# A two-layer decoder on one core: the order of the MLPs' products, the fetching of the modulation columns, operand offsets and a slot for raw weights

## The chip, the cores and the metric

The kernel runs on one core of one Trainium2 chip. The metric is the device time of one launch in microseconds (us). The engines are TensorE (PE, with its weight loads shown apart as PEld), VectorE (DVE), ScalarE (ACT), GpSimd (POOL) and SyncE (SP). SP only issues transfers, in strict order; POOL issues the transfers that add to what lies in SBUF already.

## The reference

One sequence of 512 tokens, model width 1024, two layers, everything in f32. Each layer modulates with six vectors that come from the conditioning vector `c`; layer 0 mixes with pooling windows, layer 1 with a gated unit (SGU); both end with an MLP of width 4096.

```python
c_act = jax.nn.silu(c)
for i in range(DEPTH):
    mod = c_act @ ada_w[i] + ada_b[i]
    sh1, sc1, g1, sh2, sc2, g2 = jnp.split(mod, 6, axis=-1)
    h = modulate(rmsnorm(x, norm_mix_g[i]), sh1, sc1)
    y = pool_mixer(h, ...) if i == 0 else sgu_mixer(h, ...)
    x = x + g1[:, None, :] * y
    h = modulate(rmsnorm(x, norm_mlp_g[i]), sh2, sc2)
    x = x + g2[:, None, :] * (jnp.square(jax.nn.relu(h @ mlp_w1[i])) @ mlp_w2[i])
return rmsnorm(x, final_g)
```

## The kernel before

**Split products.** TensorE works on f32r operands. Each f32 operand is split in a high part (`wh`, an ACT copy, L181) and a low part (`wl`, the rest, a DVE subtraction, L182), and each product is three matmuls: low by high, high by low, high by high (`mm3`, L194). So every weight block of 128 x 1024 costs one ACT and one DVE operation before PE can use it. Activations are split in the same way (L633 and L634).

**Seven products instead of eight.** Both matrix products of an MLP, M1 (`h @ w1`) and M2 (`... @ w2`), are cut in 2 x 2 blocks and computed in a Strassen-like way, with seven products numbered 1 to 7 in place of eight. Sums and differences of blocks are the operands. For the weights they are made one from another: a block `ch` (M1) or `bt` (M2) is loaded, split, then another block is added to it, and it is split again. DVE makes some of these additions (L742), the others are transfers that POOL issues (L738, L833). Results of the seven products are accumulated in PSUM, in two banks: 1, 6, 7, 4 in the X bank, 5 and 3 in the Z bank, 2 in a bank of its own (in M2, one that takes the Z bank's place once 3 is done). Between products of one bank, the sum so far has to be read out (L770 to L778 in M1). So product 4 may not begin before DVE has read the X bank after product 7 (L776).

**M1** runs over four columns `c` and two halves `j`. A unit `("s", (c, j, m))` is product m of group (c, j), 24 matmuls of 256 columns. Group (c, j) needs the blocks (0,0) (`ch`, slots T0 and T1), and (0,1), (1,1), (1,0) (`raw`, from the pool w4 with three buffers, which the modulation columns use too). The products run in the order 1, 5, 6, 3, 7, 2, 4, group after group, with the first groups interleaved. In layer 0 the first seven blocks of 128 columns, and block 7, are computed without this scheme while the normalisation is still running (the sweep).

**M2** runs over four blocks `c` of the hidden width. A unit `("p", (c, m))` is product m of block c: 24 matmuls of 512 columns, weights (stationary) from `o`, the split activations, and moving operands `wh`, `wl`. Here product m runs for c = 0..3 before the next m. Blocks: (0,0) is `bt`, (1,1) is `b` (slots P2, P3 in layer 0), (1,0) is `raw`.

**Order of the work.** PE follows the list `us` exactly. The other engines' instructions are traced up to five units ahead of the product that needs them (a unit of M2 counts as two) and then put in order by a scheduler, which moves them by its own estimates. `blk` loads a raw block when its product is BLK = 3 units ahead.

**Modulation columns.** `mod` is computed by columns: a 128 x 1024 tile `ada` of the weights is fetched (L210) and DVE multiplies it with the broadcast `c` and sums along the row (L214, one `ada_tile`). The gate of the MLP (eight columns) is turned to a row and broadcast by a trip through DRAM into `gb`, 128 x 1024 (`spread_cols`). In layer 0, 8 + 6 columns run during M1 through the slots T20 and T21, one every 2.2 products from the eighth on; ten more come during M2 through w4. In layer 1 eight columns are listed for M1. Fetch and use of a column are traced at the same place, and the scheduler may move both.

**Offsets.** Weight parts `wh`, `wl` lie at an address that is 192 modulo 512 bytes, activations at 128 modulo 512: `shift(big, 16)` puts 16 words between them. So in every product the two operands are 64 bytes apart.

```python
def shift(pool, words):
    if words % LINE:
        pool.tile([P, words % LINE], F32, name="shift", tag=f"shift{len(shifts)}", bufs=1)
```

Of the kernel before, what the change touches and what calls it, by code (L numbers as in the profile page):

```python
# [14 lines left out]
P = 128  # L15
# [12 lines left out]
PAD = 112  # L28

BLK = 3  # L30

EX = 6

EXW, EXE = 8, 2.2
# [49 lines left out]
def decoder_kernel(ctx: ExitStack, tc: tile.TileContext, xtok, vecs, rows, fgrow, ada0, adag, ada1, pool_w, w1s, w1f, w1b, w2, w_v, w_u, w_o, wsT, lnp, bs, out):  # L84
# [59 lines left out]
    gb = big.tile([P, D], F32, name="gb", tag="gb")  # L144
    shift(big, 16)
# [24 lines left out]
    def wtile(tag, dt=F32R):  # L170
        return wts.tile([P, D], dt, name=tag, tag=tag)

    def wpair():
        return wtile("wh"), wtile("wl")

    def split(r, n=1):

        h, l = wpair()
        for q in range(n):
            c = slice(D // n * q, D // n * (q + 1))  # L180
            A.activation(h[:, c], r[:, c], AF.Copy)  # L181
            V.tensor_tensor(l[:, c], r[:, c], f32(h[:, c]), ALU.subtract)  # L182
        return h, l
# [23 lines left out]
    def ada_tile(i, t, src, get):  # L207

        r = get()
        nc.sync.dma_start(r, src)  # L210
        b, j = divmod(t, 2)
        if j == 0:
            pmv[i, b] = sm.tile([P, 2], F32, name="pmv", tag="pmv")
        V.scalar_tensor_tensor(r, r, 1.0, cb, ALU.mult, ALU.mult, accum_out=pmv[i, b][:, j : j + 1])  # L214
# [17 lines left out]
    def spread_cols(cols, name):  # L232
# [7 lines left out]
        G.dma_start(gb, line.rearrange("(o k) p -> o (k p)", o=1).to_broadcast([P, D]))  # L240
# [25 lines left out]
    with (  # L266
# [90 lines left out]
        def load(name):  # L357
            kind, d = name.rstrip("0123456789"), [int(c) for c in name if c.isdigit()]
            for j, (pool, tag) in enumerate(places(name)):
                r = pool.tile([P, D], F32, name="ada", tag=tag) if pool is w4 else wtile(tag, F32)  # L360
# [255 lines left out]
    shift(late[0], PAD)  # L616

    ORDER = (1, 5, 6, 3, 7, 2, 4)
# [47 lines left out]
    def mlp(i, extra, wait, every, units, final):  # L666
# [5 lines left out]
        TS = ["T0", "T2", "T1", "R2"]  # L672
# [50 lines left out]

        def blk(c, j, r, n):
            if (c, j, r, n) not in blks:
                blks[c, j, r, n] = raw4(w1b[i, 2 * c + j, r, n], f"raw{c}{j}{r}{n}q")
            return blks[c, j, r, n]

        more = {}

        def s_prep(u):
# [14 lines left out]
            w = split(wb)  # L746
            if m == 6:
                add(t, *CHAIN[4])
            for at in more.get(u, ()):
                blk(*at)  # L750
            return w
# [36 lines left out]
        def t_load(c):  # L788
            if c == 3:
# [15 lines left out]

        def p_prep(u):
# [14 lines left out]
            o = slot(f"R{c % 2}", [P, 2, 4, 2, P], "o", F32R)  # L821
# [16 lines left out]
        XB, ZB = {}, {}  # L838

        def p_run(u, ready):  # L840
            c, m = u
            o, w = ready
            banks = XB if m in IN_X else ZB
# [5 lines left out]
            for n in range(8):  # L849
                p, hf = (n % 4, n // 4) if end else (n // 2, n % 2)  # L850
                wv = cut(w[p // 2], ALL, slice(S * (p % 2), S * (p % 2) + S))
                if (end and i and hf):
                    continue
                mm3(banks[hf], cut(o, ALL, p, hf), wv, start and p == 0, stop and p == 3, skip_group_check=True)
                if end and p == 3 and hf == 0:
# [15 lines left out]
            for hf in range(2):  # L871
# [5 lines left out]
                elif m in (3, 7):  # L877
                    with tc.high_priority():
                        V.tensor_tensor(yt, yt, banks[hf], ALU.subtract if m == 7 else ALU.add)
                else:  # L880
                    final(t, dh, 0, S, banks[hf], yt)
# [9 lines left out]
        ss_ = [u for k, u in units if k == "s"]  # L891
        need = {}
        for n, (c, j, m) in enumerate(ss_):
            for at in {2: [(c, j, 1, 0)], 5: [(c, j, 0, 1)], 6: [(c, j, 1, 1)]}.get(m, []):
                need.setdefault(at, n)
        for at, n in need.items():
            if n >= BLK:
                more.setdefault(ss_[n - BLK], []).append(at)
        real = [n for n, (k, u) in enumerate(units) if k in prep]
        ready = {}  # L900
        extra, n_s, total = list(extra), 0, len(extra)
        for n, (kind, u) in enumerate(units):
# [8 lines left out]
            for m in real[x:]:  # L911
                s += items[units[m][0]]
                if s > 5 and m != n:
# [3 lines left out]
            if kind == "s":  # L917
                n_s += 1
                while extra and n_s >= wait + every * (total - len(extra)):
                    extra.pop(0)()  # L920
# [4 lines left out]
    def gated(t, c0, n, src, y=None):  # L925
        tmp = sm.tile([P, S], F32, name="tmp", tag="tmp")[:, 0:n]
# [3 lines left out]
        V.tensor_tensor(tmp, src if y is None else y, gb[:, c0 : c0 + n], ALU.mult)  # L930
# [15 lines left out]
    def normed(hf, i, n):  # L946
# [13 lines left out]
        for k in range(0, KD, 2):  # L960
# [4 lines left out]
            tt = h32[k // 4][:, k % 4 : k % 4 + 2, c] if i and n else sm.tile([P, 2, 256], F32, name="tt", tag="tmp")  # L965
            for q in range(2):
                a, b = scl[i][n][:, k + q : k + q + 1], mod(i, c_sh(n, k + q))
                if q:
                    A.activation(tt[:, q], px[:, 256:512], AF.Identity, bias=b, scale=a)
# [9 lines left out]
    def p_units():  # L979
# [4 lines left out]
        us += [("p", (0, 2)), ("xl", (0,)), ("xl", (1,)), ("p", (1, 2)), ("sum", (0, 1)), ("sum", (1, 1)), ("p", (2, 2)), ("p", (3, 2))]  # L984
        us += [("p", (0, 4)), ("sum", (2, 1)), ("sum", (3, 1)), ("p", (1, 4)), ("p", (2, 4)), ("p", (3, 4))]
        return us

    def spread(i, name):
        return lambda: spread_cols(mods[i][:, c_g(1, 0) : c_g(1, 0) + KD], name)
# [5 lines left out]
    def ada_slot(t):  # L995
        return lambda: slot(f"T2{t % 2}", [P, D], "ada")

    ex = [lambda q=q: ada_tile(0, 40 + q, ada1[q], ada_slot(q)) for q in range(8)]
    ex += [lambda q=q: ada_tile(1, q, ada1[8 + q], ada_slot(q)) for q in range(EX)]
# [3 lines left out]
    us += s_units(2, 0, ORDER[1:]) + s_units(2, 1) + s_units(3, 0) + s_units(3, 1)  # L1003
    after(us, ("s", (2, 1, 2)), ("x", spread(0, "gain0")))
    after(us, ("s", (3, 1, 3)), ("tl", (0,)))
    us += p_units()
    after(us, ("p", (1, 4)), ("x", lambda: normed(0, 1, 0)))
    at = us.index(("p", (1, 5)))
    for q in range(EX, 16):
        us.insert(at + 1, ("x", lambda q=q: ada_tile(1, q, ada1[8 + q], get4)))  # L1010
        at += 2
    mlp(0, ex, EXW, EXE, us, lambda t, dh, c0, n, src, y: gated(t, S * dh + c0, n, src, y))
# [235 lines left out]
```

## Time and profile before

| | us |
|---|---|
| median of 3 runs (range) | 894.78 (888.55 to 895.37) |
| profiled execution | 896.06 |
| its span | 894.4 |

| stage | from, to (us of the span) |
|---|---|
| modulation and pool mixer | 0 to 60 |
| sweep, block 7 | 60 to 106 |
| M1 of layer 0 | 106 to 235 |
| M2 of layer 0 | 235 to 410 |
| SGU mixer, output projection last | 410 to 558 |
| M1 of layer 1 | 558 to 726 |
| M2 of layer 1 | 726 to 885 |

The mean granted clock of TensorE is 0.982. 188.62 MB are moved, 211 GB/s in the mean. The profile's rows are read so: a group's row has the line, engine, operation, out<-in and count, then busy time and mean duration; a row of waits has who waited for whom with total, times and longest; a row of the timeline has start, length, engine, line and operation, and in brackets the idle time before it and what ended it; a row of stretches has the busy time of each engine, the granted clock, the DMA share and GB/s.

### The profile page before, as it was taken

The page shows a single profiled execution, that of the slowest core. Times are in us where ns is not written, and L with a number is a line of the kernel's source. Part 1 is how long each engine was busy: PE and PEld are TensorE (multiplying, and loading weights), DVE is VectorE, ACT ScalarE, POOL GpSimd, SP SyncE. Part 2 cuts the span into 40 slices and gives each one's busy share as a digit, 9 for nine tenths or more (in the row PEclk, how much of TensorE's full clock was granted, in tenths as well). Part 3 has the DMA queues.
Part 4 walks back from the last instruction along what each step waited for, and adds up shares of the span by engine and source line. Part 5 has one row for each costly group of instructions (what it writes and reads, how often), then busy time and mean ns, then how long its engine had stood idle before and what let it go on. Part 6 is the DMA issues. An engine that isn't in the chain of part 4 may idle for free.

```text
span 894.4 us, 12710 instructions
## 1 busy us (share of the span) xinstructions
PE 845.1 (94%) x4895; PEld 738.2 (83%) x4895; DVE 693.5 (78%) x886; ACT 512.2 (57%) x732; POOL 110.5 (12%) x137
## 2 busy tenths in 40 slices
PE   8999999899849999999999989898999999999995
PEld 6778899899738888878888868898999998888884
DVE  5889789866939867687798975894766678966885
ACT  4286876567525555566331424774766675555661
POOL 3010010010213310020020001110101022311000
PEclk9999999999969999999999999999999999999998
DMA  9989969876999988336658864557566799998411
GB/s 343 407 329 309 303 150 264 256 208 198 292 264 204 202 191 206 121 105 242 209 191 272 282 224 164 166 136 194 148 153 183 198 252 223 206 195 188 165 48 47
DMA packets 51650, 188.62 MB, mean 211 GB/s; under 512 B 5739, under 2 KB 5891, under 8 KB 50566
## 3 DMA queue, kind: packets, MB, share of 16 engines
q1 hardware_dynamic: 37090, 133.52, 41.9%
q0 software_dynamic: 14352, 54.02, 31.4%
q8 instruction: 38, 0.62, 0.3%
q10 hardware_dynamic: 148, 0.27, 0.1%
q14 instruction: 22, 0.18, 0.1%
HBM read 181.49 MB, written 6.30 MB: 210 GB/s over the span
## 4 chain that ended last, share of the span: by engine, by line
PE 51%; DVE 20%; DMA 17%; ACT 5%; issue 4%; POOL 1%; SPq 1%; POOLq 0%; DVEq 0%; ACTq 0%
PE pm L194 29%; DMA ada<-in_ada 7%; DVE wl L182 5%; DVE ada L214 3%; PE po L194 3%; PE b211q L194 2%; PE b301q L194 2%; DMA wh<-in_ada 2%; PE b311q L194 2%; DMA ch10q<-in_w1b 2%; PE b201q L194 2%; ACT wh L181 2%; DVE ada L393 1%; PE b101q L194 1%; PE b111q L194 1%
## 5 line engine op out<-in xcount | busy, mean ns | idle before, releaser
L194 PE MATMUL pm<-wh,o 128*128 128x512 f32 (+1 forms) x904 | 284.4, 396 | 13.5 <-DVE o L634 13.0
L194 PEld LDWEIGHTS pm<-wh,o 128*128 128x128 f32 x904 | 171.1, 190 | 53.1 <-DVE o L634 13.4
L194 PE MATMUL pm<-wl,o 128*128 128x512 f32 (+1 forms) x452 | 179.1, 396 | 1.1 <-DVE wl L182 1.1
L634 DVE TENSOR_TENSOR o<-g,o 128x1024 fp32r<-128x1024 f32 x56 | 68.5, 1224 | 44.8 <-ACT o L633 44.6
L194 PEld LDWEIGHTS pm<-wl,o 128*128 128x128 f32 x452 | 85.8, 190 | 21.2 <-ACT tmp L935 1.5
L633 ACT ACTIVATE o<-g 128x1024 fp32r<-128x1024 f32 x56 | 59.3, 1058 | 71.5 <-PE pm L194 69.7
L214 DVE SCALAR_TENSOR_TENSOR ada<-ada,cb 128x1024 f32<-128x1024 f32 x56 | 67.9, 1222 | 34.2 <-DMA ada<-in_ada 34.0
L181 ACT ACTIVATE wh<-bt 128x1024 fp32r<-128x1024 f32 x64 | 67.3, 1054 | 32.9 <-PE pm L194 32.3
L182 DVE TENSOR_TENSOR wl<-bt,wh 128x1024 fp32r<-128x1024 f32 x64 | 78.5, 1236 | 5.2 <-ACT wh L181 5.1
L194 PE MATMUL po<-hb,wh 128*128 128x512 f32 x224 | 70.4, 395 | 0.0
L833 POOL DMA_DIRECT2D bt<-in_w x48 | 40.9, 852 | 130.0 <-DVE wl L182 124.1
L194 PEld LDWEIGHTS po<-hb,wh 128*128 128x128 f32 x224 | 42.1, 188 | 9.9
L182 DVE TENSOR_TENSOR wl<-raw,wh 128x1024 fp32r<-128x1024 f32 x33 | 40.2, 1223 | 8.6 <-ACT wh L181 8.6
L181 ACT ACTIVATE wh<-raw 128x1024 fp32r<-128x1024 f32 x33 | 34.7, 1053 | 19.6 <-DMA raw<-in_w_o 7.7
L194 PE MATMUL po<-hb,wl 128*128 128x512 f32 x112 | 44.8, 400 | 1.0 <-ACT g L696 1.0
L182 DVE TENSOR_TENSOR wl<-b,wh 128x1024 fp32r<-128x1024 f32 x32 | 39.0, 1222 | 5.3 <-ACT wh L181 5.3
L194 PE MATMUL po<-wh,gt 128*128 128x512 f32 x128 | 41.8, 405 | 0.0
L688 ACT ACTIVATE g<-g 128x512 f32<-128x512 f32 (+1 forms) x72 | 40.6, 596 | 1.3
L181 ACT ACTIVATE wh<-b 128x1024 fp32r<-128x1024 f32 x32 | 33.8, 1055 | 11.6 <-PE pm L194 11.0
L194 PE MATMUL po<-wh,hb 128*128 128x512 f32 x128 | 40.1, 392 | 0.0
L935 ACT ACTIVATE tmp<-x 128x512 f32<-128x512 f32 (+1 forms) x25 | 15.2, 608 | 40.9 <-DVE x L931 40.8
L780 ACT ACTIVATE g<-g 128x512 f32<-128x512 f32 x42 | 26.1, 622 | 20.1 <-DVE g L774 12.9
(438 smaller groups left out, 1992.8 us busy)
## 6 DMA issues: line engine op xcount, KB each, us to landing
ada<-in_ada SPq DMA_DIRECT2D x72, 512.0 KB, 4.7
bt<-in_w POOLq DMA_DIRECT2D x48, 512.0 KB, 9.1
bt<-in_w SPq DMA_DIRECT2D x16, 512.0 KB, 4.7
b<-in_w SPq DMA_DIRECT2D x16, 512.0 KB, 5.6
raw<-in_w SPq DMA_DIRECT2D x16, 512.0 KB, 4.3
b<-in_w POOLq DMA_DIRECT2D x16, 512.0 KB, 6.6
wh<-in_ada SPq DMA_DIRECT2D x9, 512.0 KB, 9.7
wl<-in_ada SPq DMA_DIRECT2D x9, 512.0 KB, 9.7
```

The lines of the kernel that those rows point to most:

```text
L181: A.activation(h[:, c], r[:, c], AF.Copy)
L182: V.tensor_tensor(l[:, c], r[:, c], f32(h[:, c]), ALU.subtract)
L194: T.matmul(o[:, c], a, b[:, c], start=first and q == 0 and not c.start, stop=last and q == 2 and c.stop is None, **kw)
L214: V.scalar_tensor_tensor(r, r, 1.0, cb, ALU.mult, ALU.mult, accum_out=pmv[i, b][:, j : j + 1])
L393: V.scalar_tensor_tensor(r, r, 1.0, cb, ALU.mult, ALU.mult, accum_out=out)
L633: A.activation(o[0], a, AF.Copy)
L634: V.tensor_tensor(o[1], a, f32(o[0]), ALU.subtract)
L688: A.activation(t, t, AF.Square)
L780: A.activation(t, t, AF.Relu)
L833: G.dma_start(r, piece(c, *nxt, q), accum_op=ALU.add)
L935: A.activation(tmp, xt, AF.Square, scale=D**-0.5, accum_out=s[:, len(cs) : len(cs) + 1])
```

## The change

1. *M2's order.* Product 2 is no longer behind 7 but spread over the list, with a bank of its own for all of M2 (`WB`); `o` takes the slots R0 and R1 in turn of use; loads of `b` move behind product 6 of block 1; block 2 of `bt` takes R2 and block 3 takes T1. Within a product the terms run high by high, low by high, high by low over all of a block's four pairs, not three terms pair by pair. The residual sums move.
2. *M1's order.* 1, 5, 6, 3, 2, 7 and then product 1 of the next group ahead of 4. In layer 1 the two halves of columns 0 and 1 alternate.
3. *Columns.* Fetch and use are two steps at given units: in layer 0 from unit 3 on, one every 1.8 units, used three units after the fetch (20 columns in M1, the last four from unit 61 on through w4); in layer 1 one every two units from unit 20 on. Both steps keep their place in the program's order.
4. *Raws in the gate row's slot.* Block (1,0) of a group, and in layer 1 (1,1) of two groups, goes to `gb`'s slot in place of w4. `spread_cols` takes the slot back during M2. LEAD = 4 in place of BLK = 3.
5. *Offsets.* The shifts between the pools go. Buffers of `wh`, `wl` have 64 words more, so they start at 128 or 384 modulo 512 bytes, the activations at 128; for M1 alone (`UNDER`) the weights lie 16 words further. So M2, the sweep and the mixer have their operands 0 or 256 bytes apart (modulo 512), M1 64 or 320.
6. Smaller: `tmp` has two buffers instead of three, the layers' second normalisations run at high priority and on ACT alone.

```diff
-PAD = 112
-BLK = 3
-EX = 6
-EXW, EXE = 8, 2.2
+UNDER = 16
+LEAD = 4
+EX = 12
+EXW, EXE, EXP, LAG, AHEAD = 3, 1.8, 61, 3, 5
...
-    gb = big.tile([P, D], F32, name="gb", tag="gb")
-    shift(big, 16)
+    gbs = [big.tile([P, D], F32, name="gb", tag="gb")]
...
-        return wts.tile([P, D], dt, name=tag, tag=tag)
+        return wts.tile([P, D + 64], dt, name=tag, tag=tag)
+    def wpair(at=0):
+        return tuple(wtile(tag)[:, at : at + D] for tag in ("wh", "wl"))
...
-    ORDER = (1, 5, 6, 3, 7, 2, 4)
+    ORDER = (1, 5, 6, 3, 2, 7)
...
+        def in_gb(c, j, r, n):
+            return ((r, n) == (1, 0) and (i, c, j) != (1, 0, 0)) or (i, r, n, j) == (1, 1, 1, 1) and c < 2
...
-            w = split(wb)
+            w = split(wb, 1, UNDER)
...
-            if c == 3:
+            if c == 2:
                 t = slot("R2", [P, 2, D], "bt")
...
-            for n in range(8):
-                p, hf = (n % 4, n // 4) if end else (n // 2, n % 2)
+            if not end:
+                for q in range(2):
+                    for n, (a, b) in enumerate(((0, 0), (1, 0), (0, 1))):
+                        for p in range(2):
+                            for hf in range(2):
+                                T.matmul(banks[hf], o[a][:, 2 * q + p, hf], w[q][b][:, S * p : S * p + S], start=start and q + n + p == 0, stop=stop and q + n + p == 4, skip_group_check=True)
...
-        us += [("p", u) for u in ((0, 3), (1, 3), (0, 7), (1, 7), (2, 3), (3, 3), (2, 7), (3, 7))]
-        after(us, ("p", (1, 5)), ("bl", (0,)), ("bl", (1,)))
+        us += [("p", u) for u in ((0, 3), (1, 3), (1, 2), (0, 7), (1, 7), (2, 3), (3, 3), (2, 2), (2, 7), (3, 7), (3, 2))]
+        us.insert(4, ("p", (0, 2)))
+        after(us, ("p", (1, 6)), ("bl", (0,)), ("bl", (1,)))
...
+            def fetch(src=src, tag=tag, r=r):
+                r.append(slot(tag, [P, D], "ada") if tag else get4())
+                tc.keep_in_program_order(nc.sync.dma_start(r[0], src))
+            def column(i=i, t=t, r=r):
+                ada_column(i, t, r[0], tc.keep_in_program_order)
+            extra.setdefault(int(when(n)), []).append(fetch)
+            extra.setdefault(int(when(n)) + (LAG if tag else 2), []).insert(0, column)
```

What it makes of the engines' orders is shown at three places. The first is DVE at the seam from M1 to M2 of layer 0, where the first `o` (low part of the first M2 operand) stands. Before:

```order
L214 SCALAR_TENSOR_TENSOR ada_2654,pmv_2656<-ada_2654,cb_104 128x1024
L182 TENSOR_TENSOR wl_2223<-raw3110q_2128,wh_2222 128x1024
L214 SCALAR_TENSOR_TENSOR ada_2661,pmv_2656<-ada_2661,cb_104 128x1024
L182 TENSOR_TENSOR wl_2258<-ch31q_1503,wh_2257 128x1024
L199 TENSOR_TENSOR mods1_90<-pmv_2656,vec_78 128x2
L214 SCALAR_TENSOR_TENSOR ada_2669,pmv_2671<-ada_2669,cb_104 128x1024
L203 SCALAR_TENSOR_TENSOR scl10_93<-mods1_90,vec_78 128x1
L634 TENSOR_TENSOR o_2317<-g_898,o_2317 128x1024
L182 TENSOR_TENSOR wl_2321<-bt_2313,wh_2320 128x1024
```

And now:

```order
L181 TENSOR_TENSOR wl_2270<-ch31q_1516,wh_2269 128x1024
L217 SCALAR_TENSOR_TENSOR ada_2176,pmv_2273<-ada_2176,cb_104 128x1024
L181 TENSOR_TENSOR wl_2335<-bt_2327,wh_2334 128x1024
L638 TENSOR_TENSOR o_2402<-g_896,o_2402 128x1024
L791 TENSOR_TENSOR g_1719<-b315q_2243,g_1719 128x512
L638 TENSOR_TENSOR o_2331<-g_896,o_2331 128x1024
L181 TENSOR_TENSOR wl_2340<-bt_2328,wh_2339 128x1024
L793 TENSOR_TENSOR g_1791<-g_1791,b311q_2178 128x512
L217 SCALAR_TENSOR_TENSOR ada_2241,pmv_2273<-ada_2241,cb_104 128x1024
```

Three columns stood in a row of seven operations ahead of the first `o`; now one stands ahead and one behind it.

The second is SP's queue at the same seam (`b` is the block of products 3 and 7, `bt` of the others, `raw` of product 2). Before:

```order
L795 DMA bt_2498<-in_w2 128x1024 x2
L795 DMA bt_2458<-in_w2 128x1024
L210 DMA ada_2711<-in_ada1 128x1024
L210 DMA ada_2757<-in_ada1 128x1024
L210 DMA ada_2799<-in_ada1 128x1024
L210 DMA ada_2842<-in_ada1 128x1024
L804 DMA b_2658<-in_w2 128x1024 x2
L804 DMA b_2666<-in_w2 128x1024 x2
L210 DMA ada_2884<-in_ada1 128x1024
L210 DMA ada_2929<-in_ada1 128x1024
L210 DMA ada_2971<-in_ada1 128x1024
```

And now:

```order
L166 DMA raw_3000<-in_w2 128x1024
L1037 DMA ada_2241<-in_ada1 128x1024
L812 DMA bt_2474<-in_w2 128x1024 x2
L812 DMA bt_2405<-in_w2 128x1024
L812 DMA bt_2515<-in_w2 128x1024
L812 DMA bt_2406<-in_w2 128x1024
L821 DMA b_2875<-in_w2 128x1024 x2
L821 DMA b_2878<-in_w2 128x1024 x2
L166 DMA raw_3006<-in_w2 128x1024
L821 DMA b_3048<-in_w2 128x1024 x2
L821 DMA b_3087<-in_w2 128x1024 x2
L1037 DMA ada_3166<-in_ada1 128x1024
```

Seven column fetches stood among these blocks; now one stands ahead of them and the next behind all four loads of `b`.

The third is DVE at the output projection of the SGU mixer (`po` is its PSUM bank, `wl` the split of its weights; ada_5605 and up are the eight columns of layer 1's MLP gate, ada_4495 and ada_4494 the last one of the mixer's own). Before:

```order
L182 TENSOR_TENSOR wl_4574<-raw_4571,wh_4573 128x1024
L1091 TENSOR_TENSOR gt_4410<-u_3991,gt_4410 128x512
L214 SCALAR_TENSOR_TENSOR ada_5670,pmv_5607<-ada_5670,cb_104 128x1024
L214 SCALAR_TENSOR_TENSOR ada_5740,pmv_5742<-ada_5740,cb_104 128x1024
L199 TENSOR_TENSOR mods1_90<-pmv_5607,vec_78 128x2
L214 SCALAR_TENSOR_TENSOR ada_5811,pmv_5742<-ada_5811,cb_104 128x1024
L930 TENSOR_TENSOR tmp_4490<-po_4446,gb_105 128x512
```

And now:

```order
L181 TENSOR_TENSOR wl_4573<-raw_4570,wh_4572 128x1024
L1132 TENSOR_TENSOR u_3989<-po_4402,u_3989 128x512
L1131 TENSOR_TENSOR po_4412<-po_4412,wsbs_3629 128x512
L1137 TENSOR_TENSOR gt_4409<-u_3989,gt_4409 128x512
L1132 TENSOR_TENSOR u_3989<-po_4412,u_3989 128x512
L1137 TENSOR_TENSOR gt_4409<-u_3989,gt_4409 128x512
L951 TENSOR_TENSOR tmp_4489<-po_4445,gb_4132 128x512
```

The gate's columns are gone from this place; they stand in layer 1's M1 now.

More of the change, by code (lines that the diff above doesn't have):

```diff
@@ L895, in mlp @@
                 need.setdefault(at, n)
+        spare[:] = [at for at in need if in_gb(*at)]
         for at, n in need.items():
-            if n >= BLK:
-                more.setdefault(ss_[n - BLK], []).append(at)
+            if not in_gb(*at):
+                more.setdefault(ss_[max(n - LEAD, 0)], []).append(at)
         real = [n for n, (k, u) in enumerate(units) if k in prep]
         ready = {}
-        extra, n_s, total = list(extra), 0, len(extra)
         for n, (kind, u) in enumerate(units):
@@ L916, in mlp @@
                     ready[m] = prep[units[m][0]](units[m][1])
[L917 to L920, printed above, removed]
+            for f in extra.get(x, ()):
+                f()
             run_[kind](u, ready[n])
@@ L1147, in last1 @@
             nc.sync.dma_start(out[t, :, 0], xt[:, 0:S])
-    ex = [lambda q=q: ada_tile(1, 40 + q, ada1[48 + q], ada_slot(q)) for q in range(8)]
+    ex = columns([(1, 40 + q, ada1[48 + q], f"T2{q % 2}") for q in range(8)], lambda n: 20 + 2 * n)
     def h_late():
```

133 lines of the change are left out of this document (78 added, 55 removed).

## The prediction

> **What bounds the kernel now.** I read the page first, for the engine that is busiest, then the table of stretches, to see in which stages that engine is not busy.
>
> ```profile
> PE 845.1 (94%) x4895; PEld 738.2 (83%) x4895; DVE 693.5 (78%) x886; ACT 512.2 (57%) x732; POOL 110.5 (12%) x137
> ```
>
> ```profile
> 106.00:235.00 129.00, 121.54 (x1012) 120.22 (x1011) 106.62 (x133) 86.73 (x125) 13.01 (x16) 0.97 0.79 229
> 235.00:268.00 33.00, 20.04 (x83) 16.09 (x83) 17.34 (x24) 11.30 (x13) 5.70 (x7) 0.80 0.97 267
> 268.00:395.00 127.00, 127.00 (x545) 102.89 (x544) 101.80 (x103) 73.57 (x81) 23.54 (x25) 1.00 0.76 173
> 560.00:726.00 166.00, 158.62 (x1343) 157.57 (x1343) 120.80 (x120) 115.36 (x161) 19.50 (x23) 0.99 0.66 174
> 726.00:872.00 146.00, 146.00 (x630) 118.32 (x628) 114.87 (x111) 86.58 (x96) 26.27 (x31) 1.00 0.77 178
> ```
>
> The columns are the stretch, its length, then busy time and count of PE, PEld, DVE, ACT and POOL, the granted PE clock, the DMA share and GB/s. TensorE is the bound. In M2 (268 to 395 and 726 to 872) it never stops. It stops in M1 of both layers (106 to 235, 560 to 726) and hardest at the seam between M1 and M2 of layer 0 (235 to 268), where the clock falls too. So I look next at what PE waits for, and what DVE waits for.
>
> ```profile
> PE pm L194 <- DVE o L634: 13.0, 1, 13.0
> PE b201q L194 <- DVE g L776: 3.1, 1, 3.1
> ...
> PE b011q L194 <- ACT g L770: 2.7, 1, 2.7
> PE b311q L194 <- DVE g L776: 2.6, 1, 2.6
> PE b101q L194 <- ACT g L770: 2.6, 2, 2.3
> PE po L194 <- DVE wl L182: 2.5, 1, 2.5
> PE px L964 <- ACT xs L952: 2.1, 2, 1.7
> PE b012q L194 <- ACT h L969: 2.0, 1, 2.0
> ```
>
> ```profile
> DVE ada L214 <- DMA ada<-in_ada: 34.0, 14, 14.3
> ...
> DVE ch10q L742 <- DMA raw1011q<-in_w1b: 4.9, 1, 4.9
> DVE ch11q L742 <- DMA raw1111q<-in_w1b: 4.5, 1, 4.5
> ```
>
> Each row is who waited for whom: total us, times, longest. PE's longest waits are for DVE or ACT; DVE's own longest waits are for transfers, and an engine that waits holds everything behind it. A wait also costs after it has ended, since the clock is low for a while:
>
> ```profile
> 169.00:173.00 4.00, 3.96 (x20) 3.96 (x21) 4.00 (x7) 3.95 (x6) 0.00 (x0) 0.57 0.79 224
> 231.00:235.00 4.00, 4.00 (x22) 4.00 (x23) 4.00 (x7) 3.30 (x5) 0.85 (x1) 0.60 1.08 223
> 264.50:268.50 4.00, 3.62 (x9) 2.90 (x10) 4.00 (x8) 0.00 (x0) 1.71 (x2) 0.52 0.58 164
> 534.00:538.00 4.00, 3.75 (x9) 2.83 (x10) 4.00 (x6) 0.64 (x1) 0.00 (x0) 0.57 0.71 250
> 571.00:575.50 4.50, 4.50 (x26) 4.50 (x27) 3.61 (x6) 3.44 (x7) 0.20 (x1) 0.63 0.82 154
> ```
>
> At the usual 0.113 us (M1) or 0.233 us (M2 and the mixer) a matmul, these 20, 22, 9, 9 and 26 matmuls would take 2.3, 2.5, 2.1, 2.1 and 2.9 us. The low clock therefore costs about 1.7, 1.5, 1.5 (after 0.4 us of the wait that still lies inside), 1.7 and 1.5 us.
>
> The Trainium skill, page "TensorE: Matmul & The Clock Gate", section "HAM oscillation — how this bites in real kernels", says that the clock is throttled by idle gaps longer than about 3.4 us. By that rule only the 13.0 us wait would cost clock, the other four drops would stay, and the sum below would end about 4 us higher, near 866. The rows speak against it: the clock is at 0.57 to 0.63 after waits of 3.1, 2.6, 2.5 and 2.0 us.
>
> **The change part by part.** The sum is made against the profiled execution's 896.1 us (its span of 894.4 and 1.7 around it). That is 1.3 us above the median, and I leave this difference out.
>
> *The seam of layer 0 (columns fetched early and pinned).* The timeline of DVE there:
>
> ```profile
> 243.56 2.47 DVE L182 TENSOR_TENSOR wl<-bt,wh 128x1024 fp32r<-128x1024 f32 x2
> 245.95 0.15 DVE L203 SCALAR_TENSOR_TENSOR scl<-mods,vec 128x1 f32<-128x1 f32 x1
> 260.38 1.23 DVE L214 SCALAR_TENSOR_TENSOR ada<-ada,cb 128x1024 f32<-128x1024 f32 x1 [14.28 <-DMA ada<-in_ada]
> ...
> 263.60 1.22 DVE L634 TENSOR_TENSOR o<-g,o 128x1024 fp32r<-128x1024 f32 x1
> ```
>
> ```profile
> 237.14 5.72 SPq L210 DMA_DIRECT2D ada<-in_ada  x3
> ```
>
> SyncE issues the last three ada transfers only from 237.1, behind four w2 blocks for product 3, and DVE sits on one of them for 14.28 us; the low part `o`, for which PE waits 13.0, is two ada columns behind it. In the new order two columns stand at this seam, fetched before those blocks, and the last four come eighteen products later. The wait has nothing left to wait for: 13.0 plus 1.5 of clock. What is late next is the first low part itself. M2's new term order needs it only after the four matmuls of the high parts, so I keep 0.5 us and take **-14**. If the cover fails (a column that is late again), up to the whole 14 comes back.
>
> *M1 of layer 0.* Here the waits are not for transfers but for DVE's turn:
>
> ```profile
> 165.43 0.68 DVE L774 TENSOR_TENSOR g<-b205q,g 128x512 f32<-128x512 f32 x1
> 166.03 1.22 DVE L214 SCALAR_TENSOR_TENSOR ada<-ada,cb 128x1024 f32<-128x1024 f32 x1
> ...
> 167.17 1.22 DVE L182 TENSOR_TENSOR wl<-ch21q,wh 128x1024 fp32r<-128x1024 f32 x1
> 168.30 0.68 DVE L776 TENSOR_TENSOR g<-g,b201q 128x512 f32<-128x512 f32 x1
> ```
>
> PE may start product 4 only when L776 has read product 7 from the same bank, and two long operations are ahead of it. The change spaces the columns evenly, fetches each three products before its use, and puts two products instead of one between 6 and 7 (between 7 and 4 it stays one). That removes at most 3.1 + 2.6 and 0.3 (b101q's shorter wait) plus 1.7 + 1.5 of clock, 9.2. But the load stays: 106.62 us of DVE in a stretch that would shrink from 129 to about 120, or 89%. At such a load some evictions are late still; I take two thirds, **-6**. The other side: at 1.22 us a column, two more than now in this stretch, uncovered, are +2.5.
>
> *The gate row's slot for M1's raws, and the new product order in M1 of layer 1.*
>
> ```profile
> ACT wh L181 <- DMA ch10q<-in_w1b: 7.7, 2, 4.9
> ...
> ACT wh L181 <- DMA ch01q<-in_w1b: 4.7, 1, 4.7
> ```
>
> ACT waits 4.7 and 4.9 us at a split for a block to which GpSimd's transfer is still adding, DVE at the same time 4.9 and 4.5 us for a raw, and the copies that free PE's bank stand behind these splits: PE waits 2.7 and 2.3. A fourth buffer for raws (the gate row's) and a lead of four products instead of three bring the raws earlier. Interleaved pairs of groups put six or seven products instead of three between product 6, which starts the addition, and product 4, which needs it. I take 4.5 of these 5.0. The start of this stage (b012q 2.0, 1.5 of clock) gets the normalisation at high priority, but both halves of it on ACT: half, 1.7. Together **-6.2**. In exchange eight columns of 1.22 us come into this stage; DVE has 120.80 of 166, so 45 us of room hide them. Without that cover they would cost 10.
>
> *The mixer's output projection.* The first of the same eight columns now stand in front of it, hoisted there:
>
> ```profile
> 523.52 1.23 DVE L214 SCALAR_TENSOR_TENSOR ada<-ada,cb 128x1024 f32<-128x1024 f32 x1 [4.35 <-DMA ada<-in_ada]
> ```
>
> They delay the split that `po` waits for (2.5, then 1.7 of clock). With them gone from there I take **-4**.
>
> *M2's product order.* Both M2 stretches show PE busy throughout, so the order of products and of the terms within one can gain nothing inside them: **0**. The cover is DVE's slack, 25 of 127 us in the one and 31 of 146 in the other; w2 blocks for product 2 are loaded earlier, but each still has several products of 5.6 us. At the end of layer 0's M2 the normalisation now stands ahead of two residual sums; the px row's 1.7 us is there, and I take **-1.2**.
>
> *The address offset.* Profile rows cannot show a pair of operands at the same offset: in the kernel before, every product has 64 bytes between them. They do show that the pace isn't one number:
>
> ```profile
> 236.00:251.00 15.00, 15.00 (x67) 12.33 (x66) 0.00 (x0) 0.00 (x0) 1.00 1.05 274
> 270.00:394.00 124.00, 124.00 (x533) 100.42 (x532) 3.83 (x6) 3.60 (x6) 1.00 0.75 172
> ...
> 107.00:126.00 19.00, 19.00 (x164) 1.00 0.68 190
> 175.00:227.00 52.00, 52.00 (x460) 1.00 0.74 209
> 628.00:683.00 55.00, 55.00 (x469) 1.00 0.63 166
> ```
>
> ```profile
> 35.65 3.62 PE L470 MATMUL po<-pw,pd 128*128 128x256 f32 x16
> ```
>
> The first two rows are M2's own matmuls (512 columns): about 0.229 us each ahead of the long wait (one or two of the 67 straddle the edges) and 0.233 behind it. The next three, 256 columns in M1, give 0.116, 0.113 and 0.117: about 4% between two paces at the same offsets, and the pace changes only where PE has stood. The last row, of two-pass f32, has 15 steps in 3.62 less 0.38 for the last one's tail, 0.216 a step. The offset changes for some 1,344 matmuls of M2 (56 products of 24) and 768 in the sweep and the mixer. Bounds: all at 0.216 would give 2,112 x 0.017 = -36 us; a loss twice as large as the one that 0.233 has against 0.216 would give +36. I stay near M2's own rows and count only that fewer long waits leave more of it at the faster pace: **-2**.
>
> The Trainium skill, page "SBUF — State Buffer", section "Who interferes with whom", gives the streamed operand and the weight load two independent read ports. By that the offset cannot matter, this term is 0, and the sum is 864; no run here shows it yet.
>
> Sum: 14 + 6 + 6.2 + 4 + 1.2 + 2 = 33.4; 896.1 - 33.4 = 862.7, so **862**.
>
> **The rivals.** *Only the seam and the projection are won.* For it speaks DVE's 89%: M1's evictions may wait as before, and pinned columns can no longer slide behind them. Against it, the stretch of 175 to 227 ran without a wait. It gives 896 - 14 - 4 = 878, up to 888 if two added columns and a slow pace (+4% of 100 us) come on top.
>
> *The common offset is the faster one.* At 0.226 a step (twice M1's fast 0.113) 2,112 matmuls save 15 instead of 2: 849; at 0.216 it is 828. For it: a slow pace exists and nothing else in the rows explains it. Against: M1 keeps its 64 bytes and has both paces.
>
> *The common offset collides (the slower side).* If a weight load and a stream that start in step disturb each other, each of the 2,112 steps pays. The price decides from 33.4 / 2,112 = 0.016 us, 7% of a step. At +0.017 the time is 900, and with M1 not improved, 914. Against it: the two paces differ by half of that.
>
> *The change doesn't do what it says:* the columns' transfers could still wait in SyncE's queue behind blocks whose slots DVE must free. Then the seam stays and the time is near 885.
>
> **How the numbers follow.** Forecast (850 to 876) 0.60; seam and projection only 0.14; fast offset 0.11; collision 0.12; queue as before 0.03. The range takes in the fast offset's nearer half and the partial win: 842 to 888; outside remain the far half of the one and most of the collision. About 1% (9 us) is what a measurement of this kernel can tell from no change. Faster by more: forecast, fast offset, nearly all of the partial win, 0.82. Within 1%: a mild collision and the rest, 0.07. Slower: 0.11.
>
> **What would show it.** Right: no DVE wait for ada above 2 us between 100 and 250; PE's wait for the first `o` under 1 us and no low clock there; no wait of `po` for `wl` in the projection; raw waits in layer 1 gone; M2 still without a gap. Wrong: M2's 533 or so matmuls in 124 us become fewer than 510 or more than 560 (the offset), or L776's successor ends waits of 2 to 3 us in M1 again (DVE's load).

## The result, and the profile after

The changed kernel takes **860.65 us** in the median (857.71 to 864.85, four runs), the kernel before 893.88 in the runs beside it: a ratio of 0.9642, 95% interval 0.9581 to 0.9703. The forecast was 862. The profiled execution took 864.85 (span 863.1) and is the slowest of the four; the one of before, 896.06, lay 2.2 above its median. Their difference is 31.2, against a sum of 33.4.

The first line of the page after, and the stretches that answer to those shown of before (columns as there: PE, PEld, DVE, ACT, POOL, clock, DMA share, GB/s):

```profile
PE 836.9 (97%) x4895; PEld 737.4 (85%) x4895; DVE 690.0 (80%) x878; ACT 514.9 (60%) x740; POOL 117.9 (14%) x137
```

```profile
106.00:226.50 120.50, 118.59 (x1009) 117.99 (x1008) 108.11 (x137) 85.07 (x124) 11.20 (x13) 1.00 0.85 252
226.50:250.00 23.50, 21.65 (x95) 17.29 (x94) 15.03 (x13) 13.33 (x15) 5.26 (x7) 1.00 1.04 262
250.00:372.00 122.00, 120.39 (x529) 98.56 (x529) 100.36 (x103) 72.57 (x81) 23.41 (x26) 1.00 0.81 194
372.00:392.00 20.00, 17.08 (x71) 14.04 (x70) 15.02 (x20) 12.77 (x19) 8.33 (x3) 0.83 0.66 226
...
534.00:575.00 41.00, 36.48 (x303) 35.50 (x302) 34.35 (x38) 34.54 (x53) 4.68 (x5) 1.00 0.45 118
575.00:700.00 125.00, 125.00 (x1064) 125.00 (x1063) 96.26 (x103) 86.86 (x118) 12.98 (x15) 1.00 0.84 230
700.00:842.00 142.00, 142.00 (x628) 117.47 (x628) 114.17 (x109) 85.20 (x95) 27.74 (x33) 1.00 0.78 183
```

The seam (235 to 268 before, now 226.5 to 250) has lost its hole: PE stands 1.85 us in it where it stood 13. Up to 842 the clock is 1.00 but for one stretch, 372 to 392. M1 of layer 1 stands only in its first 41 us. New is that M2 of layer 0 has gaps (120.39 of 122, then 17.08 of 20). By stages, with the boundaries of the table ahead and those of the new trace (106, 226.5, 391.7, 534.4, 699.9, 853.9):

| stage | before | after | change | forecast (offset shared out by steps) |
|---|---|---|---|---|
| M1 of layer 0 | 129 | 120.5 | -8.5 | -6 |
| M2 of layer 0 | 175 | 165.2 | -9.8 | -15.8 |
| SGU mixer | 148 | 142.7 | -5.3 | -4.5 |
| M1 of layer 1 | 168 | 165.5 | -2.5 | -6.2 |
| M2 of layer 1 | 159 | 154.0 | -5.0 | -0.6 |

The waits of PE, and then those of DVE and ACT for transfers:

```profile
PE pm L874 <- DVE o L638: 3.1, 3, 1.4
PE px L985 <- ACT xs L973: 2.9, 2, 2.4
PE b001q L193 <- DVE wl L181: 1.6, 1, 1.6
PE b002q L193 <- DVE sums L960: 1.6, 1, 1.6
...
PE b101q L193 <- DVE g L793: 1.2, 1, 1.2
```

```profile
DVE ada L217 <- DMA ada<-in_ada: 3.1, 4, 1.1
...
DVE ch11q L757 <- DMA raw1111q<-in_w1b: 2.6, 1, 2.6
DVE ch10q L757 <- DMA raw1001q<-in_w1b: 2.4, 1, 2.4
...
ACT wh L180 <- DMA raw<-in_w: 0.7, 1, 0.7
```

DVE's waits for columns fell from 34.0 (longest 14.3) to 3.1 (1.1). No wait of `po` for `wl` is left. The raws' waits are halved, not gone. The normalisation's wait (`px`) at the end of layer 0's M2 grew from 1.7 to 2.9 (2.4, then 0.6), and it is what costs clock:

```profile
375.60:382.40 6.80, 6.23 (x23) 0.51 0.59 207
537.00:541.00 4.00, 2.40 (x21) 1.00 0.87 328
```

After the 2.4 us wait the clock is at half for 6.8 us, which costs about 3 (eight matmuls of M2 take 3.27 us there and 1.98 at full clock); after the wait of 1.6 us at 537 it stays at 1.00. But the length of a wait doesn't decide it. Four of the kernels below have the same pair of waits at this place (2.3 to 2.4 us, then 0.6 or 0.7): behind it the clock was at half for 6.8 us (M1 at 128 bytes), for 3.4 (the offset undone; M1's old order in layer 1) or not at all. This is the stretch of the last one, M1 at 0 or 256 bytes; its 15 transposes `px` took 1.86 us there, 3.46 in the changed kernel:

```profile
376.00:383.00 7.00, 6.22 (x35) 1.00 0.72 237
```

In the kernel before, too, waits of 2.7 and 2.3 us in M1 of layer 1 left the clock at 1.00. The rule of the Trainium skill that the prediction weighed ("TensorE: Matmul & The Clock Gate", section "HAM oscillation — how this bites in real kernels": idle gaps over about 3.4 us) would have no loss in this kernel; the row of 375.60 above is against it.

### The profile page after: what moved, and what is told of

Its sections match the earlier page's. It is cut to its first block, busy times and chain, and to the rows that moved or that the text cites. A ratio compares the mean times of both kernels' runs of the same rounds, so it can differ in the third digit from the quotient of the medians.

```text
span 863.1 us, 12746 instructions
## 1 busy us (share of the span) xinstructions
PE 836.9 (97%) x4895; PEld 737.4 (85%) x4895; DVE 690.0 (80%) x878; ACT 514.9 (60%) x740; POOL 117.9 (14%) x137
## 4 chain that ended last, share of the span: by engine, by line
PE 58%; DVE 19%; DMA 12%; issue 5%; ACT 4%; POOL 1%; SPq 0%; POOLq 0%; DVEq 0%; ACTq 0%
PE pm L874 28%; PE po L193 6%; DVE wl L181 4%; DVE ada L217 3%; PE b211q L193 3%; PE b301q L193 3%; DMA wh<-in_ada 2%; PE b201q L193 2%; PE b311q L193 2%; DMA ada<-in_ada 2%; DVE ada L397 2%; ACT wh L180 1%; PE b111q L193 1%; PE b205q L193 1%; PE b305q L193 1%
## 5 line engine op out<-in xcount | busy, mean ns | idle before, releaser
L874 PE MATMUL pm<-wh,o 128*128 128x512 f32 x864 | 216.1, 392 | 3.8 <-DVE o L638 3.1
L874 PEld LDWEIGHTS pm<-wh,o 128*128 128x128 f32 x864 | 162.4, 189 | 39.6 <-DVE o L638 4.3
L874 PE MATMUL pm<-wl,o 128*128 128x512 f32 x432 | 115.7, 389 | 0.1
L874 PEld LDWEIGHTS pm<-wl,o 128*128 128x128 f32 x432 | 81.0, 188 | 17.4 <-DVE wl L181 0.5
L181 DVE TENSOR_TENSOR wl<-raw,wh 128x1024 fp32r<-128x1024 f32 x33 | 40.2, 1221 | 14.3 <-ACT wh L180 14.2
```

Source lines behind the costliest of these rows:

```text
L874: T.matmul(banks[hf], o[a][:, 2 * q + p, hf], w[q][b][:, S * p : S * p + S], start=start and q + n + p == 0, stop=stop and q + n + p == 4, ...
```

## The experiments

Theory to begin with: the sum of the prediction, except that its offset term is too small, since M2's steps now have one steady pace (745 to 820, PE busy throughout: before 323 matmuls, after 332).

**The offset undone, and the offset alone.**

```diff
-    def wpair(at=0):
+    def wpair(at=16):
...
-    def split(r, n=1, at=0):
+    def split(r, n=1, at=16):
```

> The changed kernel with one thing undone: all weight parts lie 16 words further again, so that M2, the sweep and the mixer have 64 or 320 bytes between their operands (modulo 512), as M1 has. Theory (the common offset gives M2 its steady 0.2267 us a step): M2 and the mixer go back to 0.229 to 0.233 a step, and 2,100 steps at 0.0025 to 0.0065 more give 866 to 874 us instead of 861. Rival (the pace comes from the new term order, or from PE no longer standing before M2): still 0.2267 a step, 861 us.

> The kernel before with part 5 of the change alone (and two buffers of tmp instead of three, to make room): operands of M2, the sweep and the mixer 0 or 256 bytes apart, M1 at 64 or 320. Theory: 0.2267 a step in M2 and the mixer instead of 0.233, 10 us less, 884 us, with PE's waits for the first o (13.0) and for wl (2.5) still there. Rival (the pace comes from the new term order or the missing long wait): 0.233 behind the 13 us wait as before, 893 us.

```diff
-    shift(big, 16)
...
-        return wts.tile([P, D], dt, name=tag, tag=tag)
...
+        return wts.tile([P, D + 64], dt, name=tag, tag=tag)
...
-    shift(late[0], PAD)
...
-            w = split(wb)
+            w = split(wb, 1, 16)
```

Measured: undone, 861.31 us (858.58 to 866.25; 0.9665 of before, 0.9600 to 0.9731); alone, 890.15 (0.9972, 0.9942 to 1.0002). The theory fell in its time: no difference in the first, and at most 5 us in the second, perhaps nothing. The paces it speaks of are there, though. The same stretches of before and of the offset alone (M2 alone), of the offset undone, and after:

```profile
745.00:820.00 75.00, 75.00 (x323) 1.00 0.99 199
```

```profile
745.00:820.00 75.00, 75.00 (x332) 1.00 0.99 205
```

```profile
165.00:220.00 55.00, 55.00 (x487) 1.00 0.87 284
585.00:680.00 95.00, 95.00 (x841) 1.00 0.85 242
...
745.00:820.00 75.00, 75.00 (x329) 1.00 0.76 182
```

```profile
165.00:220.00 55.00, 55.00 (x469) 1.00 0.89 274
585.00:680.00 95.00, 95.00 (x809) 1.00 0.83 231
...
745.00:820.00 75.00, 75.00 (x332) 1.00 0.83 195
```

Counts in equal time are paces: M2 (745 to 820) at 0.232, 0.226, 0.228 and 0.226. The offset alone gives the old kernel the pace of the changed one, with the old terms and the old order. With 64 bytes between the operands M2 has two paces, and the profiled run of the undone kernel happened on the better one. M1 (165 to 220, 585 to 680) has the same 64 bytes in the last two kernels, yet runs at 0.113 in the one and 0.117 in the other: 4 ns on 2,352 steps are some 9 us, as much as the offset gives. In the kernel with the offset alone M2 took 3.8 us less in layer 0 and 3.7 in layer 1, and what stands ahead of layer 0's M2 took 3.8 more. PE also waits more for the others there (before: 2.6 us for this eviction, 3.1 for that of `b201q`, now 3.8, and 13.0 for `o`):

```profile
PE pm L193 <- DVE o L632: 11.6, 1, 11.6
PE b311q L193 <- DVE g L774: 4.5, 1, 4.5
```

**M1 at other distances.**

```diff
-UNDER = 16
+UNDER = 0
```

> The changed kernel with UNDER = 0: M1's weights lie at the activations' offset as well, 0 or 256 bytes apart. Theory (a common offset is what gives the fast pace): M1's 0.1175 us a step becomes its fast 0.113 throughout; about 1,750 steps that now take 0.1175 give 8 us less, 853 us. Rival (M1's two paces have nothing to do with the offset): both paces as now, 861 us. Second rival (M1 loses at a common offset): steps above 0.1175, over 865 us.

The second kernel has `UNDER = 32`.

> The changed kernel with UNDER = 32: M1's operands 128 or 384 bytes apart instead of 64 or 320. Theory (only 0 modulo 256 is special; any other distance has two paces, set anew at each stop): M1 at 113.3 and 117.8 ns a step again, 861 us within the spread. Rivals: a steady pace at 113.3, 853 us; or a steady 120.0 as with 0 or 256 bytes, 867 us.

Measured: 866.85 us (0.9730, 0.9661 to 0.9799) and 865.24 (two runs; 0.9694, 0.9631 to 0.9758). The first theory fell the other way, to its second rival; at 128 bytes neither the theory's two paces nor one of the rivals' was met. M1 with 0 or 256 bytes:

```profile
165.00:220.00 55.00, 55.00 (x460) 1.00 0.86 261
585.00:680.00 95.00, 95.00 (x794) 1.00 0.81 228
```

That is 0.120 throughout, more than either pace at 64 bytes. With 128 or 384 bytes it was in between (466 and 803, 0.118). So a common offset gives 512 columns their best pace and 256 columns their worst. The Trainium skill, page "SBUF — State Buffer", section "Who interferes with whom", gives the streamed operand and the weight load independent read ports. By that there would be no effect at all. Here nothing but the weights' address in M1 differs, and M1's pace does. The times differ by less than their intervals; it is the counts that show it.

**M2's terms pair by pair again.**

```diff
-                for q in range(2):
-                    for n, (a, b) in enumerate(((0, 0), (1, 0), (0, 1))):
...
+                for n in range(8):
+                    p, hf = n // 2, n % 2
+                    mm3(banks[hf], cut(o, ALL, p, hf), ...)
```

> The changed kernel with M2's terms pair by pair again (three terms for each of the eight pairs), everything else as changed. Theory (the order of the terms is worth nothing inside M2, only the first product of a stage waits a little more for the low part of o): pace 0.2267, 0 to 3 us more, 861 to 864 us. Rival (the term order makes the pace): 0.233 a step, 870 us.

Measured: 862.67 us (0.9669, 0.9609 to 0.9730), with 332 matmuls from 745 to 820 as after. The theory held: the order of the terms makes no pace. M1's code and addresses are those of the changed kernel, and its paces in this run were one of each:

```profile
165.00:220.00 55.00, 55.00 (x487) 1.00 0.90 284
585.00:680.00 95.00, 95.00 (x808) 1.00 0.83 233
```

**The columns alone.** Before, with the columns of the change: `EX = 12`, fetch and use at fixed units, pinned.

```diff
-EX = 6
-EXW, EXE = 8, 2.2
+EX = 12
+EXW, EXE, EXP, LAG = 3, 1.8, 61, 3
...
+    ex = columns(cols, lambda n: EXW + EXE * n if n < 8 + EX else EXP + n - 8 - EX)
```

> The kernel before with part 3 of the change alone (columns fetched three products ahead, at fixed units, pinned; 20 in layer 0's M1, eight in layer 1's M1). Theory: the 13.0 us wait at the seam and its clock go (14), the wait of po for wl in the output projection and its clock go (4), M1 of layer 0 with two more columns keeps its waits for DVE: 893 - 18 = 875 us, 871 to 880. Rival (the seam's gain needs M2's new order and terms, or two more columns delay M1's evictions more): a wait over 5 us is left at the seam or new waits over 2 us in M1, 885 us or more.

Measured: 899.54 us, slower than before (1.0090, 1.0052 to 1.0127). The theory fell. The seam is mended (at most 1.6 us of wait for `o`), and the time is lost again a hundred microseconds on. What ACT and PE wait for, and SyncE's queue (its start, how long it stood at that group, what it issued):

```profile
ACT wh L181 <- DMA raw<-in_w: 23.5, 6, 6.3
...
PE pm L194 <- ACT wh L181: 8.7, 3, 4.2
...
PE pm L194 <- DVE o L638: 2.8, 2, 1.6
```

```profile
235.00 79.53 SPq L808 DMA_DIRECT2D b<-in_w  x7
314.58 0.43 SPq L1004 DMA_DIRECT2D ada<-in_ada  x1
315.12 1.11 SPq L167 DMA_DIRECT2D raw<-in_w  x2
332.12 5.32 SPq L255 DMA_DIRECT2D x<-xd  x2
341.18 0.33 SPq L1004 DMA_DIRECT2D ada<-in_ada  x1
342.92 6.85 SPq L167 DMA_DIRECT2D raw<-in_w  x2
...
```

The last four columns of layer 0 stand in the queue behind the loads of `b`, which wait for their slots until 314. Then they take turns with the raws of product 2 in w4's three buffers, and in the old list the four products 2 follow one another, two raws each 5.6 us. ACT waits for six of these eight raws, and PE twice 4.2 us behind it.

**The same, with those four columns left as before** (the cut is against the run above).

```diff
-    cols = [(*c, f"T2{n % 2}" if n < 8 + EX else None) for n, c in enumerate(cols)]
-    ex = columns(cols, lambda n: EXW + EXE * n if n < 8 + EX else EXP + n - 8 - EX)
+    cols = [(*c, f"T2{n % 2}") for n, c in enumerate(cols[: 8 + EX])]
+    ex = columns(cols, lambda n: EXW + EXE * n)
...
+    at = us.index(("p", (1, 5)))
+    for q in range(EX, 16):
+        us.insert(at + 1, ("x", lambda q=q: ada_tile(1, q, ada1[8 + q], get4)))
+        at += 2
```

> The kernel before with 20 columns pinned in layer 0's M1 and eight in layer 1's M1, as in the first run of the columns alone, but the last four of layer 0 placed as in the kernel before (behind product 5 of block 1 in M2, not pinned). Theory (those four took the w4 buffers from the eight raws of product 2, which in the old order come four products in a row, and PE stood for them): the seam's 13 us gone, no wait over 2 us of ACT for a raw in M2 of layer 0, 893 - 18 = 875 us, 871 to 881. Rival (M2 in its old order cannot keep pace once the stop ahead of it is gone, wherever the columns go): waits of about 4 us in M2's second half again, 890 us or more.

Measured: 877.43 us (0.9819, 0.9754 to 0.9884): 17 less than before, where the theory said 18. ACT no longer waits for raws of M2. By stages of the profiled runs M2 of layer 0 took 9.9 us less and the mixer 4.0; another 3.4 lie ahead of and in the two M1. At the seam a wait of 3.0 for `o` is left (the second row), with half clock behind it. In M1 of layer 0 the columns alone mend nothing: its waits are no longer at `b201q` and `b311q` (column 2, half 0 and column 3, half 1, X bank), but at `b301q` and `b101q`.

```profile
PE b301q L194 <- ACT g L774: 3.5, 1, 3.5
PE pm L194 <- DVE o L638: 3.0, 1, 3.0
...
PE b101q L194 <- DVE g L780: 2.3, 1, 2.3
```

**The old list of M2's products in the changed kernel.**

```diff
-        us += [("p", u) for u in ((0, 3), (1, 3), (1, 2), (0, 7), (1, 7), (2, 3), (3, 3), (2, 2), (2, 7), (3, 7), (3, 2))]
-        us.insert(4, ("p", (0, 2)))
-        after(us, ("p", (1, 6)), ("bl", (0,)), ("bl", (1,)))
+        us += [("p", u) for u in ((0, 3), (1, 3), (0, 7), (1, 7), (2, 3), (3, 3), (2, 7), (3, 7))]
+        after(us, ("p", (1, 5)), ("bl", (0,)), ("bl", (1,)))
+        us += [("p", (0, 2)), ("xl", (0,)), ("xl", (1,)), ("p", (1, 2)), ("sum", (0, 1)), ("sum", (1, 1)), ("p", (2, 2)), ("p", (3, 2))]
...
```

> The changed kernel with the old list of M2's products in both layers (product 2 of the four blocks in a row behind product 7), terms, banks and everything else as changed. Theory (the new list is what leaves w4's buffers to both the columns and the raws of product 2): waits of 2 to 4 us of PE in M2 of layer 0 with half clock behind them, 6 to 12 us more, 867 to 873 us. Rival (the prediction's term of 0 for the order of M2's products): 861 us.

Measured: 877.94 us (0.9818, 0.9776 to 0.9861), 17 more than after, beyond the theory's 12. PE's and ACT's waits are those of the columns alone:

```profile
PE pm L874 <- ACT wh L180: 11.3, 4, 5.1
```

```profile
ACT wh L180 <- DMA raw<-in_w: 24.0, 6, 5.9
```

In the changed kernel ACT's waits for these raws are 0.7 in all (the last row shown of it). PE's two long waits here, 4.9 and 5.1, lie in M2 of layer 0. The new list is what makes room for the pinned columns; the loads of `b` went back with it, behind product 5, and the two weren't separated. Nor was the old list tried in the changed kernel with the last four columns left unpinned; in the kernel before, that combination had no such wait.

**The gate row's slot alone**, in the kernel before:

```diff
-BLK = 3
+LEAD = 4
-                blks[c, j, r, n] = raw4(w1b[i, 2 * c + j, r, n], f"raw{c}{j}{r}{n}q")
+                if in_gb(c, j, r, n):
...
-    after(us, ("s", (2, 1, 2)), ("x", spread(0, "gain0")))
+    after(us, ("p", (1, 5)), ("x", spread(0, "gain0")))
```

> The kernel before with part 4 alone (block (1,0), and (1,1) of two groups, in the gate row's slot, a lead of four products instead of three, the gate rows spread during M2), with the old orders of products. Theory: DVE's waits of 4.9 and 4.5 us for raws in layer 1 and PE's waits behind them (b011q 2.7, b101q 2.3, with some clock) go: 4 to 5 us less, 889 us; the seam of layer 0 stays at 13 us. Rival (not the slot but the interleaved order of products, which gives the adding transfers more time, removes them): the two PE waits stay above 1.5 us each, 893 us.

Measured: 882.28 us (0.9897, 0.9841 to 0.9953), 9 less, but not where the theory put it:

```profile
PE pm L194 <- DVE o L635: 5.2, 1, 5.2
...
PE b011q L194 <- ACT g L783: 2.7, 1, 2.7
...
PE b112q L194 <- DVE wl L182: 2.3, 1, 2.3
```

In layer 1 DVE's waits of 4.9 and 4.5 for raws are gone (one of 1.5 grew to 4.0), but `b011q` waits 2.7 as before, and where `b101q` waited 2.3 `b112q` now does. The gain is in M2 of layer 0, 9.0 us: at the seam no wait for `o` is left, since SyncE issued the last eight columns of M1 ahead of the blocks `b`, where some stood behind them before. That the raw which left w4 is why they came forward is likely, not shown.

```profile
204.71 12.05 SPq L210 DMA_DIRECT2D ada<-in_ada  x4
...
224.03 9.54 SPq L210 DMA_DIRECT2D ada<-in_ada  x4
234.79 2.60 SPq L817 DMA_DIRECT2D b<-in_w  x4
```

The wait of 5.2 is a new one, at 312 to 317, far behind the seam. PE and ACT there:

```profile
317.66 0.79 PE L194 MATMUL pm<-wh,o 128*128 128x512 f32 x1 [5.18 <-DVE o L635]
```

```profile
311.62 1.06 ACT L181 ACTIVATE wh<-b 128x1024 fp32r<-128x1024 f32 x1 [8.55 <-DMA b<-in_w]
```

ACT waits for a block `b` to which POOL's transfers add, and DVE's `o` stands behind that split. POOL had issued nothing from 273.4 to 285.2, between the gate row's way out to DRAM and back, which part 4 moves into M2, and then issued seven additions in a row. That this delayed the block is likely, not shown.

**M1's old order**, in layer 0 (last three groups) and in layer 1.

```diff
-    us += rest(2, 0)
+    us += s_units(2, 0, O[1:]) + s_units(2, 1, O) + s_units(3, 0, O) + s_units(3, 1, O)
```

> The changed kernel with the old order 1, 5, 6, 3, 7, 2, 4 in the last three groups of layer 0's M1, where product 4 follows 7 by one product in both, but 7 follows 3 at once again and 1 of the next group comes behind 4. Theory (the order takes part in removing PE's waits for DVE in M1): waits of 2 to 3 us for the eviction L793 come back at two places with clock behind them, 4 to 6 us more, 865 to 867 us. Rival (the even spacing of the columns alone removed them): 861 us.

Layer 1, where `O = (1, 5, 6, 3, 7, 2, 4)` too:

```diff
-    for m in (5, 6, 3, 7):
-        us += [("s", (0, j, m)) for j in range(2)]
+    for n, (c, j) in enumerate(((0, 0), (0, 1), (1, 0), (1, 1), (2, 0))):
+        us += s_units(c, j, (5,) if c < 2 else (1,))
...
```

> The changed kernel with the old order of groups and products in layer 1's M1 (no pairs of groups side by side), the gate row's slot and the lead of four as changed. Theory (the pairs side by side give the adding transfers the time, the slot alone does not): waits of about 2.5 us at b011q and at one more place come back, with clock 5 us more, 866 us. Rival (the slot and the lead removed these waits): 861 us.

Layer 0: 865.30 us in the median of three runs (859.27 to 865.85; 0.9654, 0.9596 to 0.9712); a fourth, the profiled one, took 873.36 and isn't compared. M1's two paces can give this difference without any order, so it stays open. Layer 1: 868.01 (0.9700, 0.9649 to 0.9751), 7 above after in the median. The intervals overlap; the waits are plain:

```profile
PE b011q L193 <- ACT g L787: 3.8, 1, 3.8
...
PE b001q L193 <- DVE wl L181: 3.1, 1, 3.1
```

So in layer 1 it is the pairs of groups side by side that removed `b011q`'s wait; the slot had not. The changed kernel without the slot wasn't tried.

**The normalisation one product later.**

```diff
-    after(us, ("p", (1, 4)), ("x", lambda: normed(0, 1, 0)))
+    after(us, ("p", (2, 4)), ("x", lambda: normed(0, 1, 0)))
```

> The changed kernel with the first half of layer 1's normalisation traced one product later, behind product 4 of block 2 instead of block 1 at the end of layer 0's M2. Theory (PE waits 2.5 and 1.0 us there for xs and runs at half clock for 6.8 us only because its row statistics are late by that much): both waits under 1 us, no low clock, 6 us less, 855 us. Rival (the time then goes to the first product of the SGU mixer, whose h is late instead): a wait of 2 to 4 us for h behind it, 859 to 862 us.

Measured: 860.03 us (0.9620, 0.9564 to 0.9677): the rival's time, though not its wait for `h`. Of the two `px` waits 0.25 is left, and the first products of the SGU mixer wait for their weights' split (2.4 and 1.2) instead:

```profile
PE po L193 <- DVE gt L1137: 3.3, 2, 3.1
...
PE po L193 <- DVE wl L181: 2.4, 1, 2.4
```

The 3.1 for `gt`, late in the mixer, are in the runs of the old list and of layer 1's old M1 order too (2.9 and 3.2), and not after (0.2); no run shows why.

No version beats the changed kernel by more than its runs differ.

## Why the prediction was right, and which of its steps were not

- **Seam and projection, -14 and -4: right.** With the columns moved and the last four left alone the kernel took 17 us less (forecast for the two: 18), 9.9 of it in M2 of layer 0, where a wait of 3.0 stayed, and 4.0 in the mixer. In the changed kernel 13.0 of standing and 1.5 of clock became 1.85 of standing at full clock, 12.6 of the 14. The `o` that is late isn't the first one: in the kernel before, three products (72 matmuls) of M2 run ahead of the long wait, and now it is the third product that waits 0.45 for its high and 1.4 for its low part.
- **M2's product order, 0: the step that failed.** "PE busy throughout, so the order ... can gain nothing inside them" was read from a kernel in which PE stood 13 us ahead of M2's bulk and no column was pinned between M2's raws. In the changed kernel the old list costs 17. Two terms of the sum were taken as independent: with the columns placed as in the change, the 18 is won only with the new list, and the columns alone are a loss of 8. The prediction had named a column that is late again as the way to lose the 14; it was the raws that became late.
- **Offset, -2: the pace was mis-sized, the time was not.** The steps went to a steady 0.226; by the rows of 745 to 820, 75 / 323 less 75 / 332, that is 0.0063 on M2's 1,344, 8.5 us, and in its 0.226 the rival "the common offset is the faster one" had the right pace. The offset alone gave 7.5 in the two M2 and lost most of it elsewhere: 2.5 in all (not told from 0).
- **M1 of layer 0, -6: right in size** (-8.5), with DVE at 90% (forecast 89%). The two waits of 3.1 and 2.6 for L776 are gone, with their clock; at the two places where 0.9 and 0.6 were waited before, it is 1.2 and 0.7 now (L793). Whether the order or the columns' spacing did it is not settled; the columns without the new order left 3.5 and 2.3, the slot alone 3.4 and 2.7.
- **M1 of layer 1, -6.2: mis-sized** (-2.5), and the wrong cause first. The slot and the lead only moved PE's waits, the order removed the one of 2.7. Waits of 1.6, 1.6, 0.8 and 0.5 for sums and weights remain at its start. The pace took part: with the same M1, on its fast pace (841 matmuls where after has 809), the stage of the kernel with the offset undone took 160.5 us, not 165.5.
- **Normalisation, -1.2: wrong.** The wait of 1.7 became 2.9, with about 3 of clock behind it in the profiled run; moving it only moves the wait.

That the total came within 2 us is in part luck: 6.0 us too much were forecast for M2 of layer 0 and 3.7 too much for M1 of layer 1, against 4.4 too little in M2 of layer 1 and 2.5 in M1 of layer 0. M1's pace and the half clock behind `px`, 0 to 6.8 us long in kernels with the same wait, move the total by several us without any change there. Two sums among the rivals are off: 878 with 2.5 and 4 on top is 884.5, not 888, and 900 without M1's 6 and 6.2 is 912, not 914; neither bears on the forecast.

## What to carry to other kernels

A stage without a gap proves that its order is worth nothing for the kernel as it is, not for the one in which another part of the change puts work there: price each part in the presence of the others, above all where they share buffers or a queue. When a transfer is pinned in a strict queue, look at what it will alternate with in its pool, not only at the wait it removes. And when PE's pace differs between runs of the same instructions, 1% needs more runs than four, or the counts of matmuls in equal time.

## What was not expected of the hardware

- The pace of the split f32 products depends on the distance of the two operands (0 or 256, 64 or 320 and 128 or 384 bytes were run), and in opposite ways: at 0, 0.226 to 0.227 us for 512 columns and 0.120 for 256; at 64 there are two paces each, 0.228 or 0.232 and 0.113 or 0.117; at 128, 0.118 for 256 columns.
- At 64 bytes M1's pace changes at stops of PE, some of them only 0.1 us long, and holds in between. The same M1 has either: the kernel with the later normalisation gives PE the changed kernel's instructions up to the end of layer 0's M1, and has 487 matmuls in the 55 us from 165 on where the changed kernel has 469. No run shows what decides it.
- Half clock followed waits of 2.3 to 2.4 us for 6.8 us, for 3.4 or not at all, and a wait of 1.4 us at the seam in the run of layer 1's old M1 order for 3.4. What decides it beside the length of the wait no run here shows.
